# Thirty-nine instead of thirty-three first-product blocks made ahead, quarters dealt evenly, and the last activation emitted where its block ends

## The chip, the cores and the metric

The kernel runs on one core of a Trainium2 chip. The metric is the device time of one execution in microseconds (us), lower is better. The engines are TensorE (PE in the rows, with its weight loads as PEld), VectorE (DVE), ScalarE (ACT), GpSimd (POOL) and SyncE (SP); ACTq, SPq and POOLq are the sequencers that issue their transfers.

## The reference, cut to what matters

One encoder layer; what matters here is its last part, a retrieval layer that picks 16 of 16,384 experts for each of 1,024 tokens and each of 8 heads.

```python
def chunk(xc):                                   # a chunk of 128 tokens
    ...
    top_s, pos = lax.top_k(cand_s, PEER_TOPK)
    e = jnp.take_along_axis(cand_i, pos, axis=-1)          # which experts
    g = jax.nn.softmax(top_s, axis=-1).astype(xc.dtype)    # their gates
    u = peer_u[e]
    h = jax.nn.gelu(jnp.einsum('cd,chkd->chk', xc, u))     # first product
    return jnp.einsum('chk,chkd->cd', g * h, peer_v[e])    # second product
```

## The kernel before

The first 790 us (attention, convolution, projections, the start of the retrieval) are the same in both kernels. From there the tokens are handled in two ways.

**Gathered tokens.** The first 384 tokens (3 tiles of 128) are done by gathers: GpSimd issues an indirect load of 128 rows of `peer_u` or `peer_v` (512 KB, line 1152) and VectorE takes one product-and-sum over it (line 1185 for u, line 1197 for v). There are 768 such gathers in all. In the stretch below the token row that they are multiplied with lies in SBUF (`QB`); in the main loop it lies in PSUM (`ga`).

**Dense tokens.** The other 640 tokens go through all 16,384 experts, in 128 blocks of 128 experts. A block needs three things: H, the gelu of the first product (48 TensorE matmuls of 320 columns, as fp32 values split in a high and a low part, in groups of 12 called quarters here); the gates, which a gate group turns into a dense matrix for 4 tokens at a time (160 groups); and the second product of gated H with `peer_v`.

**The stretch made ahead** (lines 1398 to 1410, 862 to 1370 us). While the gate groups run, `ustep` (line 1343) makes the first product of some blocks ahead, one quarter of TensorE work after each gate group. A gate group is 3 matmuls of 512 columns (`gdiff`, lines 1080 to 1083), two ScalarE activations (`gprep`), 4 matmuls that show as 8 records (`gmat`, line 1098) and 4 ScalarE copies of 128 columns into `gblk` (`gevac`, line 1108). After eight groups ScalarE issues four transfers `GD<-gblk` (line 1111). There are five `gblk` buffers and four are used by each eight groups, so the next eight soon wait for those transfers to land. The H of a finished block gets its gelu in the middle of the next block (line 1241) and is written to HBM (`HDm`). K0 = 33 blocks are listed for this, spread over the 128 (set `US`); KM = K0 - 2 = 31 of them are done by `ustep`, 124 quarters, so they run out while 24 gate groups are left. The last gelu stands after the loop (line 1408). `kadv` deals VectorE's work in the same loop: the key selection first, then gathers, with a cost of GCOST = 3.0 each against a credit that grows with each step.

**The hand-over** (1364 to 1388 us). The two remaining listed blocks are made at once (96 matmuls), while SyncE loads what the main loop needs first: in its queue stand, in this order, the write of the last H (line 1409), a `peer_uT` block (line 1216), a stored H (line 1469), two gate loads (line 1449) and the first two `peer_v` blocks (line 1453). ScalarE and GpSimd split `peer_v` into `vh` and `vl`, and the main loop begins.

**The main loop** (lines 1594 to 1624, 127 rounds, 1388 to 2971 us). Round i does the second product of block i in three slots. Each slot holds a `rotate` (6 matmuls of 512 columns into `prot`, which VectorE adds to X, line 1557), one or two `accum` (3 matmuls of 512 columns each into PSUM that stays) and, by `ugroup`, one quarter of the first product of a block that was not made ahead. Then come the gathers of that slot, on VectorE behind the add. There is one `prot` buffer, so the next slot's `rotate` waits for VectorE's add. The 95 blocks that were not made ahead have 380 quarters for 381 slots.

The program order within each engine is as the code emits it; nothing reorders it.

Of the kernel before, what the change touches and what calls it, by code (L numbers as in the profile page):

```python
# [31 lines left out]
NK = 128  # L32
# [7 lines left out]
TB = 32  # L40
GCH = 4
NPERS = 4
K0 = 33
WIN = 2
NVI = 3
NO2 = 2
GPE = 1.4
GCOST = 3.0
KT = 2
GLAST = 1  # L50
FD = 2
# [20 lines left out]
def peer_block(tc, I, out):  # L72
    nc = tc.nc
    ctx = ExitStack()
    V, A, G, PE, SY = nc.vector, nc.scalar, nc.gpsimd, nc.tensor, nc.sync
# [51 lines left out]
    with ExitStack() as fr:  # L127
# [55 lines left out]
        with ExitStack() as st:  # L183
            a_ = st.enter_context(tc.tile_pool(name="A", bufs=1))
            ps = st.enter_context(tc.tile_pool(name="psA", bufs=2, space=PSUM))
# [306 lines left out]
        with ExitStack() as st:  # L492
            b_ = st.enter_context(tc.tile_pool(name="B", bufs=1))
            ps = st.enter_context(tc.tile_pool(name="psB", bufs=1, space=PSUM))
# [266 lines left out]
            for u in range(NU + 4):  # L761
                g = (u + 4) // 4
# [58 lines left out]
    TD = ND * P  # L821
    KM = K0 - KT
    SD = dram.tile([NT, P, 2 * PH, NK], F32, name="SD")
    GD = dram.tile([TD // TB, P, NK, TB], F32, name="GD")
    HDm = dram.tile([K0, P, TD], F32, name="HDm")
    HND = dram.tile([NG, P, D], F32, name="HND")
# [12 lines left out]
    up = u_.enter_context(tc.tile_pool(name="up", bufs=1))  # L839
# [41 lines left out]
    def hbank(shape, name):  # L881
        hb["n"] += 1
        return (psh if hb["n"] % 2 else psu).tile(shape, F32, name=name, tag="h", bufs=1)
# [320 lines left out]
    gat = Gather()  # L1204
    US = sorted({0, 1, 2, *(int(2 + j * (NK - 2) / (K0 - 2)) for j in range(K0 - 2))})
    UI = {c: j for j, c in enumerate(US)}
    assert len(US) == K0, len(US)
    ngat = NG * 256
# [5 lines left out]
    def uload(i):  # L1214
        raw = uu.tile([P, DC, P], F32, name="ur", tag="raw", bufs=2)
        SY.dma_start(raw[:], I["peer_uT"][i])
        RAW["u", i] = raw
# [4 lines left out]
    def usplit(i):  # L1222
        raw = RAW.pop(("u", i))
        uh = uu.tile([P, DC, P], F32R, name="uh", tag="uh", bufs=2)
        ul = uu.tile([P, DC, P], F32R, name="ul", tag="ul", bufs=2)
        split(uh[:], ul[:], raw[:], hi_eng=HE(i), lo_eng=V if i in UI and UI[i] > KM else G)
        UW[i] = (uh, ul)

    def useg(i, hps, d0, d1):
        uh, ul = UW[i]  # L1230
        for dc in range(d0, d1):
            for st3 in range(3):
                for j, (a, b) in enumerate(segs):
                    PE.matmul(hps[:, j, :b - a], (uh, uh, ul)[st3][:, dc, :], HN[(0, 1, 0)[st3]][:, dc, a:b],  # L1234
                              start=dc == 0 and st3 == 0, stop=dc == DC - 1 and st3 == 2)
        if d1 == DC:
            UW.pop(i)

    def gelu_(hps, pool, bufs):
        ho = pool.tile([P, TD], F32, name="ho", tag="ho", bufs=bufs)  # L1240
        A.activation(ho[:].rearrange("p (a b) -> p a b", a=len(segs)), hps[:, :len(segs), :SW], AF.Gelu_apprx_tanh)  # L1241
        return ho


    korder = [3, 4, 5, 0, 6, 7, 1, 2]
    ks = dict(n1=0, n2=0, gen=None, ld=0, credit=0.0, last="")
# [36 lines left out]
    def k_gat():  # L1283
        if not ks.get("gat") or not gat.ready():
            return None
        gat.adv(1)
        return GCOST

    def kstep():
        order = [("gen", k_gen), ("topk1", k_topk1), ("gat", k_gat)]  # L1290
# [9 lines left out]
    def kadv(us, dt):  # L1300
        clk["t"] += dt
        ks["credit"] = min(ks["credit"] + us, 6.0)
        while ks["credit"] > 0:
            c = kstep()
            if c is None:
                return
            if c == HOLD:
                break
            ks["credit"] -= c
# [30 lines left out]

    ust = dict(i=0, seg=0, hps=None, prev=None)

    def ustep():
        i = ust["i"]
        if i >= KM:
            return 0.0
        if i == 0 and ust["seg"] == 0:
            uload(US[0])
            uload(US[1])
            usplit(US[0])  # L1350
        sg = ust["seg"]
        if sg == 0:
            ust["hps"] = hbank([P, 2, 512], "hps")
        useg(US[i], ust["hps"], 2 * sg, 2 * sg + 2)
        if sg == 1 and ust["prev"] is not None:
            ho = gelu_(ust["prev"], up, 1)
            SY.dma_start(HDm[i - 1], ho[:])
        if sg == 1 and i < KM:
            usplit(US[i + 1])
            if i + 2 < K0:  # L1360
                uload(US[i + 2])
        ust["seg"] += 1
        if ust["seg"] == 4:
            ust["seg"] = 0
            ust["i"] += 1
            ust["prev"] = ust["hps"]
        return 1.65
# [32 lines left out]
    while True:  # L1400
# [4 lines left out]
            break  # L1405
        dt = max(dt + GPE * did, KB)
        kadv(dt, dt)
    ho = gelu_(ust["prev"], up, 1)
    SY.dma_start(HDm[KM - 1], ho[:])
    while ks["n2"] < len(korder):  # L1410
        clk["t"] += 2.0
        kstep()
# [2 lines left out]
    with ExitStack() as vs:  # L1415
# [40 lines left out]
        def vsplit(i):  # L1456
            raw = RAW.pop(("v", i))
            vh = vp.tile([P, D], F32R, name="vh", tag="vh", bufs=WIN + 1)
            vl = vp.tile([P, D], F32R, name="vl", tag="vl", bufs=WIN + 1)
            split(vh[:], vl[:], raw[:], lo_eng=G)  # L1460
            CH[i] = (vh, vl)
# [4 lines left out]
        def hload(i):  # L1466
            if i in UI and i not in HO and i < NK:
                HO[i] = hfree.pop(0)
                SY.dma_start(HO[i], HDm[UI[i]])
# [17 lines left out]
        def uhalf(i, hf, ps, d0=0, d1=DC):  # L1487
            a, b = segs[hf]
            uh, ul = UW[i]
            for dc in range(d0, d1):  # L1490
                for st3 in range(3):
                    PE.matmul(ps[:, :b - a], (uh, uh, ul)[st3][:, dc, :], HN[(0, 1, 0)[st3]][:, dc, a:b],  # L1492
                              start=dc == 0 and st3 == 0, stop=dc == DC - 1 and st3 == 2)
            if hf and d1 == DC:
                UW.pop(i)

        def ubank():
            return psv.tile([P, 512], F32, name="hps", tag="h", bufs=1)

        def ugelu(ho, hf, ps):  # L1500
            a, b = segs[hf]
            A.activation(ho[:, a:b], ps[:, :b - a], AF.Gelu_apprx_tanh)  # L1502

        def loads(i):
            if 0 <= i < NK:
                if i % GCH == 0:
                    gload(i)
                vload(i)


        ulist = [i for i in range(NK) if i not in UI]
        ug = dict(g=0, split=0, load=0, ps=None)

        def uahead():
            m = ug["g"] // 4
            if ug["split"] < min(m + 2, len(ulist)):
                usplit(ulist[ug["split"]])
                ug["split"] += 1
                if ug["load"] < len(ulist):
                    uload(ulist[ug["load"]])  # L1520
                    ug["load"] += 1

        def ugroup():
            m, q = divmod(ug["g"], 4)
            if m >= len(ulist):
                return
            i, (hf, d) = ulist[m], divmod(q, 2)
            if ug["split"] <= m:
                uahead()
            if d == 0:  # L1530
                ug["ps"] = ubank()
            uhalf(i, hf, ug["ps"], d * DC // 2, (d + 1) * DC // 2)
            if d == 1:
                if hf == 0:
                    HO[i] = hfree.pop(0)
                ugelu(HO[i], hf, ug["ps"])
            ug["g"] += 1

        def uready(i):
            while i not in UI and ulist.index(i) >= ug["g"] // 4:  # L1540
                ugroup()
# [19 lines left out]
        gat.to_psum(ga[:])  # L1561
        for i in range(KM + 2, K0):
            uload(US[i])
# [6 lines left out]
        for i in range(KM, K0):  # L1570
# [7 lines left out]
            ho = vp.tile([P, TD], F32, name="hm", tag="al", bufs=WIN + 1)[:]  # L1578
# [17 lines left out]
        for i in range(NK - 1):  # L1596
            nx = i + 1
            ng = gat0 + -(-(ngat - gat0) * min(nx, nb) // nb) - gat.nc
            gs = [0] * 3
            for j in range(ng):  # L1600
                gs[SPOTS[j % len(SPOTS)]] += 1
            hload(nx)
            if len(hfree) > 1:
                hload(i + 2)
            loads(i + 2)
            vsplit(nx)
            uahead()
            rs_ = [w for w in range(len(rot)) if i % WIN == w % WIN]
            rotate(rs_[0], i, False)
            accum(i, (0,))  # L1610
            ugroup()
            gat.adv(gs[0])
            rotate(rs_[1], i, False)
            accum(i, (1,))
            ugroup()
            uready(nx)
            amake1(nx)
            gat.adv(gs[1])
            amake2(nx)
            rotate(rs_[2], i, False)  # L1620
            accum(i, (2, 3))
            ugroup()
            gat.adv(gs[2])
            CH.pop(i - WIN, None)
        accum(NK - 1, range(len(pers)))
# [71 lines left out]
```

## Time and profile before

| | us |
|---|---|
| median of 3 runs | 3005.8 |
| lowest and highest of them | 3000.25 and 3015.49 |
| the profiled execution, its own time | 3001.72 |
| its span, first to last instruction | 2999.9 |
| TensorE busy in the span | 2796.1 (93%) |
| VectorE busy | 2464.3 (82%) |
| GpSimd busy | 1951.2 (65%) |
| ScalarE busy | 1148.3 (38%) |

Of the profiled execution 1.8 us lie around the span. Busy shares are means over stages with different limits, so the rows further down are taken stage by stage. Matmuls overlap in the records (one of 512 columns shows 0.39 us, and the next starts 0.23 us after it), so distances between starts are used for TensorE, not durations.

### The profile page before, as it was taken

The page shows a single profiled execution, that of the slowest core. Times are in us where ns is not written, and L with a number is a line of the kernel's source. Part 1 is how long each engine was busy: PE and PEld are TensorE (multiplying, and loading weights), DVE is VectorE, ACT ScalarE, POOL GpSimd, SP SyncE. Part 2 cuts the span into 40 slices and gives each one's busy share as a digit, 9 for nine tenths or more (in the row PEclk, how much of TensorE's full clock was granted, in tenths as well). Part 3 has the DMA queues.
Part 4 walks back from the last instruction along what each step waited for, and adds up shares of the span by engine and source line. Part 5 has one row for each costly group of instructions (what it writes and reads, how often), then busy time and mean ns, then how long its engine had stood idle before and what let it go on. Part 6 is the DMA issues. An engine that isn't in the chain of part 4 may idle for free.

```text
span 2999.9 us, 44538 instructions
## 1 busy us (share of the span) xinstructions
PE 2796.1 (93%) x16048; PEld 2476.5 (83%) x16048; DVE 2464.3 (82%) x4465; ACT 1148.3 (38%) x2376; POOL 1951.2 (65%) x1557
## 2 busy tenths in 40 slices
PE   7878899899999899988999999999999999999997
PEld 6767778699978788867888888888888888888886
DVE  5888998457667867874999988898999999899898
ACT  3216566243577577673222222222222222222222
POOL 2577842104445757774777777777777777777775
PEclk9999999999999999999999999999999999999999
DMA  3111000044334567576889898999899999999896
GB/s 125 51 68 36 8 1 15 31 145 131 109 122 163 205 245 265 196 288 246 340 330 344 328 347 334 339 337 355 335 338 335 354 342 340 339 339 340 331 343 230
DMA packets 296720, 710.33 MB, mean 237 GB/s; under 512 B 25265, under 2 KB 135217, under 8 KB 296369
## 3 DMA queue, kind: packets, MB, share of 16 engines
q0 software_dynamic: 110592, 402.70, 35.1%
q1 hardware_dynamic: 156800, 252.85, 25.0%
q10 hardware_dynamic: 29104, 51.91, 4.6%
q8 instruction: 126, 2.06, 0.3%
q14 instruction: 98, 0.79, 0.1%
HBM read 640.46 MB, written 66.91 MB: 236 GB/s over the span
## 4 chain that ended last, share of the span: by engine, by line
PE 50%; DVE 21%; DMA 12%; issue 8%; POOL 4%; ACT 4%; ACTq 1%; SPq 0%; POOLq 0%; DVEq 0%
PE hps L1492 12%; PE hps L1234 5%; PE prot L122 4%; PE prot L123 3%; PE prot L124 3%; DMA rows<-peer_u,ei 3%; DMA vr<-peer_v 3%; DVE y L146 3%; PE pg L1098 3%; DMA rows<-peer_v,ei 3%; DVE ga L1197 2%; PE acc L122 2%; PE acc L124 2%; PE acc L123 2%; DVE ho L1475 2%
## 5 line engine op out<-in xcount | busy, mean ns | idle before, releaser
L1492 PE MATMUL hps<-HN,uh 128*128 128x320 f32 x3072 | 682.9, 310 | 9.9 <-ACT ho L1241 5.3
L1492 PEld LDWEIGHTS hps<-HN,uh 128*128 128x128 f32 x3072 | 530.3, 188 | 42.9 <-issue 5.5
L1492 PE MATMUL hps<-HN,ul 128*128 128x320 f32 x1536 | 476.1, 310 | 0.6 <-POOL ul L119 0.6
L1197 DVE SCALAR_TENSOR_TENSOR ga<-rows,aa,ga 128x1024 f32<-128x1024 f32 x330 | 423.9, 1285 | 23.3 <-DMA rows<-peer_v,ei 16.7
L1152 POOL DMA_INDIRECT rows<-peer_u,ei x339 | 360.3, 1063 | 109.5 <-issue 57.9
L119 POOL TENSOR_TENSOR vl<-vr,vh 128x1024 fp32r<-128x1024 f32 x128 | 308.9, 2413 | 154.0 <-ACT vh L116 110.8
L1152 POOL DMA_INDIRECT rows<-peer_v,ei x330 | 325.4, 986 | 110.6 <-issue 64.1
L1185 DVE SCALAR_TENSOR_TENSOR QB<-rows,ga 128x1024 bf16<-128x1024 f32 x271 | 329.5, 1216 | 30.0 <-DMA rows<-peer_u,ei 25.8
L122 PE MATMUL prot<-vh,ah 128*128 128x512 f32 x762 | 308.3, 405 | 29.2 <-DVE X L1557 26.9
L119 POOL TENSOR_TENSOR ul<-ur,uh 128x1024 fp32r<-128x1024 f32 x127 | 323.2, 2545 | 2.6
L1557 DVE TENSOR_TENSOR X<-X,prot 128x512 f32<-128x512 f32 x384 | 262.0, 682 | 68.1 <-PE prot L124 66.7
L123 PE MATMUL prot<-vl,ah 128*128 128x512 f32 x762 | 301.2, 395 | 0.4 <-POOL vl L119 0.4
L124 PE MATMUL prot<-vh,al 128*128 128x512 f32 x762 | 297.6, 390 | 0.0
L1492 PEld LDWEIGHTS hps<-HN,ul 128*128 128x128 f32 x1536 | 289.2, 188 | 0.9 <-POOL ul L119 0.9
L1502 ACT ACTIVATE ho<-hps 128x320 f32<-128x320 f32 x128 | 55.8, 436 | 486.4 <-PE hps L1492 486.4
L1108 ACT COPY gblk<-pg 128x128 f32<-128x128 f32 x640 | 175.9, 441 | 97.0 <-PE pg L1098 72.5
L116 ACT CAST vh<-vr 128x1024 fp32r<-128x1024 f32 x128 | 133.7, 1045 | 202.1 <-DMA vr<-peer_v 193.3
L1234 PE MATMUL hps<-HN,uh 128*128 128x320 f32 x992 | 210.0, 334 | 0.0
L124 PE MATMUL acc<-vh,al 128*128 128x512 f32 x512 | 199.6, 390 | 0.0
L122 PE MATMUL acc<-vh,ah 128*128 128x512 f32 x512 | 199.6, 390 | 0.0
L123 PE MATMUL acc<-vl,ah 128*128 128x512 f32 x512 | 199.5, 390 | 0.0
L122 PEld LDWEIGHTS prot<-vh,ah 128*128 128x128 f32 x762 | 143.3, 188 | 64.6 <-DVE X L1557 44.5
(270 smaller groups left out, 6556.6 us busy)
## 6 DMA issues: line engine op xcount, KB each, us to landing
ur<-peer_uT SPq DMA_DIRECT2D x128, 512.0 KB, 4.2
vr<-peer_v SPq DMA_DIRECT2D x128, 512.0 KB, 7.8
GD<-gblk ACTq DMA_DIRECT2D x80, 512.0 KB, 5.2
gl<-GD SPq DMA_DIRECT2D x64, 640.0 KB, 8.0
wqr<-peer_wq SPq DMA_DIRECT2D x32, 512.0 KB, 3.9
HDm<-ho SPq DMA_DIRECT2D x31, 320.0 KB, 2.6
s<-SD SPq DMA_DIRECT2D x64, 128.0 KB, 2.9
ho<-HDm SPq DMA_DIRECT2D x22, 320.0 KB, 4.6
```

Source lines behind the costliest of these rows:

```text
L116: A.copy(hi, src)
L119: lo_eng.tensor_tensor(lo, src, f(hi), op=ALU.subtract)
L122: PE.matmul(ps, ah, bh, start=start, stop=False)
L123: PE.matmul(ps, ah, bl, start=False, stop=False)
L124: PE.matmul(ps, al, bh, start=False, stop=stop)
L1108: A.copy(gblk[b][k][:, :, q * 4:q * 4 + 4].rearrange("p i t -> p t i"), pg[:, :, k * w:k * w + w])
L1152: G.indirect_dma_start(out=r, out_offset=None, in_=I["peer_v" if ph else "peer_u"], in_offset=bass.IndirectOffsetOnAxis(ap=ge[t][:, k:k + ...
L1185: V.scalar_tensor_tensor(jk, r, 1.0, h, op0=ALU.mult, op1=ALU.mult, accum_out=self.hh[t][:, k:k + 1])
L1197: V.scalar_tensor_tensor(to, r, self.aa[t][:, k:k + 1], to, op0=ALU.mult, op1=ALU.add)
L1234: PE.matmul(hps[:, j, :b - a], (uh, uh, ul)[st3][:, dc, :], HN[(0, 1, 0)[st3]][:, dc, a:b], start=dc == 0 and st3 == 0, stop=dc == DC - 1 ...
L1492: PE.matmul(ps[:, :b - a], (uh, uh, ul)[st3][:, dc, :], HN[(0, 1, 0)[st3]][:, dc, a:b], start=dc == 0 and st3 == 0, stop=dc == DC - 1 and ...
L1557: V.tensor_tensor(X[:, NG + t, n:n + 512], X[:, NG + t, n:n + 512], pr, op=ALU.add)
```

## The change

K0 goes from 33 to 39, so KM goes from 31 to 37 and `ustep` has 148 quarters. `US` is spread anew, and 89 blocks stay for the main loop, with 356 quarters. A new `uslot` stands in the main loop where `ugroup` stood and calls it only when the share of quarters that is due by this slot is not yet made. The last gelu and its write move into a function `ulast`, which `ustep` calls as soon as it has no block left. Gathers that are dealt after the key selection count 2.0 against the credit instead of 3.0.

```diff
-K0 = 33
+K0 = 39
@@
 GCOST = 3.0
+GCOST2 = 2.0
@@
-        return GCOST
+        return GCOST if ks["n2"] < len(korder) else GCOST2
@@
+    def ulast():
+        if ust["prev"] is not None:
+            ho = gelu_(ust["prev"], up, 1)
+            SY.dma_start(HDm[KM - 1], ho[:])
+            ust["prev"] = None
+
     def ustep():
         i = ust["i"]
         if i >= KM:
+            ulast()
             return 0.0
@@
-    ho = gelu_(ust["prev"], up, 1)
-    SY.dma_start(HDm[KM - 1], ho[:])
+    ulast()
@@
-        ug = dict(g=0, split=0, load=0, ps=None)
+        ug = dict(g=0, split=0, load=0, ps=None, slot=0)
@@
+        def uslot():
+            ug["slot"] += 1
+            if ug["g"] < -(-4 * len(ulist) * ug["slot"] // (3 * (NK - 1))):
+                ugroup()
@@
             accum(i, (0,))
-            ugroup()
+            uslot()
```

The other two calls of `ugroup` in the round become `uslot` in the same way.

What this does to the order is seen at three places. On TensorE, the end of the stretch made ahead: `pg` is a gate group's product, `dg` and `dq` belong to the group after it, and `hps` on line 1234 (1235 after) is a quarter. Before:

```order
L1083 MATMUL dg<-selg,L_5328 128x512
L1098 MATMUL pg<-o_14199,o_14197 128x128 x4
L1098 MATMUL pg<-o_14214,o_14212 128x128 x4
L1492 MATMUL hps<-HN_5301,uh 128x320
L1492 MATMUL hps<-HN_5302,uh 128x320
```

and after the change:

```order
L1235 MATMUL hps<-HN_5301,ul 128x320 x2
L1099 MATMUL pg<-o_14566,o_14564 128x128 x4
L1235 MATMUL hps<-HN_5301,uh 128x320 x2
L1235 MATMUL hps<-HN_5302,uh 128x320 x2
L1235 MATMUL hps<-HN_5301,ul 128x320 x2
```

The last 24 groups stood alone; now a quarter of 12 matmuls stands behind each of them, the last one included.

On ScalarE at the same place, before:

```order
L1089 ACTIVATE o_14212<-dq 128x512
L1091 ACTIVATE o_14214<-dg 128x512
L1108 COPY gblk<-pg 128x4x32 x8
L1111 DMA GD<-gblk 128x1024 x4
L1241 ACT_TABLE_LOAD
L1241 ACTIVATE ho<-hps 128x640
L1144 COPY ga<-QB 128x1024
L116 CAST uh<-ur 128x1024
```

and after the change:

```order
L1090 ACTIVATE o_14564<-dq 128x512
L1092 ACTIVATE o_14566<-dg 128x512
L1109 COPY gblk<-pg 128x4x32 x4
L1242 ACTIVATE ho<-hps 128x640
L1109 COPY gblk<-pg 128x4x32 x4
L1112 DMA GD<-gblk 128x1024 x4
L1145 COPY ga<-QB 128x1024
L117 CAST uh<-ur 128x1024
```

The last gelu moved ahead of the last group's copies and of the four transfers; its table load is no longer here (there are as many table loads in all).

On TensorE in the main loop, first slot of round 5; `acc` is the `accum`, `hps` the quarter. Before:

```order
L124 MATMUL prot<-vh,al 128x512
L122 MATMUL acc_14253<-vh,ah 128x512
L123 MATMUL acc_14253<-vl,ah 128x512
L124 MATMUL acc_14253<-vh,al 128x512
L1492 MATMUL hps<-HN_5301,uh 128x320
L1492 MATMUL hps<-HN_5302,uh 128x320
```

and after the change:

```order
L125 MATMUL prot<-vh,al 128x512
L123 MATMUL acc_14619<-vh,ah 128x512
L124 MATMUL acc_14619<-vl,ah 128x512
L125 MATMUL acc_14619<-vh,al 128x512
L123 MATMUL prot<-vh,ah 128x512
L124 MATMUL prot<-vl,ah 128x512
```

The quarter between one `rotate` and the next is gone in this slot; 24 slots are like it, one in every fifth round (8 in each of a round's three places).

## Rows read from the trace of the kernel before

**Rows 1.** By stage: stretch, length, busy PE, PEld, DVE, ACT, POOL; clock, DMA share, GB/s.

```profile
862.00:1303.00 441.00, 417.11 (x2842) 376.51 (x2841) 334.16 (x1195) 311.07 (x869) 284.68 (x230) 0.99 0.60 210
1303.00:1365.00 62.00, 46.28 (x262) 33.13 (x260) 38.91 (x50) 45.31 (x141) 34.22 (x22) 0.89 0.69 250
1365.00:1388.00 23.00, 16.63 (x97) 16.28 (x97) 3.04 (x4) 9.18 (x15) 1.87 (x1) 0.85 0.77 260
1388.00:2971.00 1583.00, 1557.94 (x8361) 1380.72 (x8361) 1429.03 (x1778) 388.35 (x548) 1230.41 (x918) 1.00 0.91 337
```

**Rows 2.** TensorE in order of time: start, us, instruction, count, idle before and releaser.

```profile
1275.38 1.05 PE L1098 MATMUL pg<-o,o 128*128 128x128 f32 x8
...
1280.33 0.94 PE L1098 MATMUL pg<-o,o 128*128 128x128 f32 x7
...
1300.09 1.05 PE L1098 MATMUL pg<-o,o 128*128 128x128 f32 x8
...
1303.39 1.05 PE L1098 MATMUL pg<-o,o 128*128 128x128 f32 x8
...
1363.34 1.16 PE L1098 MATMUL pg<-o,o 128*128 128x128 f32 x8 [0.37 <-ACT o L1091]
```

**Rows 3.** Chain of work that ended last, within the lone gate groups: start, us, what.

```profile
1321.91 6.37 DMA GD<-gblk
...
1341.04 11.29 DMA GD<-gblk
...
1364.54 1.02 ACT gblk L1108 x4
```

**Rows 4.** All engines in order of time at the hand-over, 1365 to 1388 us.

```profile
1365.30 2.39 ACTq L1111 DMA_DIRECT2D GD<-gblk  x3
1367.72 1.28 ACT L1241 ACT_TABLE_LOAD   x1 [2.17 <-issue]
1369.02 0.70 ACT L1241 ACTIVATE ho<-hps 128x640 f32<-128x640 f32 x1
...
1369.82 0.87 PE L1492 MATMUL hps<-HN,uh 128*128 128x320 f32 x2 [5.32 <-ACT ho L1241]
...
1371.78 1.23 DVE L119 TENSOR_TENSOR ul<-ur,uh 128x1024 fp32r<-128x1024 f32 x1 [28.07 <-ACT uh L116]
...
1376.53 3.76 SPq L1453 DMA_DIRECT2D vr<-peer_v  x2
...
1385.84 0.31 PE L1492 MATMUL prot<-HN,ul 128*128 128x320 f32 x1
1387.70 0.47 PE L122 MATMUL prot<-vh,ah 128*128 128x512 f32 x1 [1.55 <-issue]
```

**Rows 5.** Who waited for whom in the main loop: us in total, times, longest.

```profile
DVE X L1557 <- PE prot L124: 66.7, 99, 3.5
...
PEld prot L122 <- DVE X L1557: 35.9, 64, 1.7
...
DVE ho L1475 <- ACT ho L1502: 1.8, 1, 1.8
```

**Rows 6.** Two slots of the main loop in order of time, TensorE and VectorE.

```profile
1455.24 0.46 PE L1492 MATMUL hps<-HN,uh 128*128 128x320 f32 x2
...
1455.31 0.68 DVE L1557 TENSOR_TENSOR X<-X,prot 128x512 f32<-128x512 f32 x1
...
1456.99 0.39 PE L122 MATMUL prot<-vh,ah 128*128 128x512 f32 x1
...
2592.07 1.22 DVE L1185 SCALAR_TENSOR_TENSOR QB<-rows,ga 128x1024 bf16<-128x1024 f32 x1 [1.74 <-DMA rows<-peer_u,ei]
...
2592.57 0.45 PE L1492 MATMUL hps<-HN,uh 128*128 128x320 f32 x2
...
2594.48 0.68 DVE L1557 TENSOR_TENSOR X<-X,prot 128x512 f32<-128x512 f32 x1
...
2595.21 0.50 PE L122 MATMUL prot<-vh,ah 128*128 128x512 f32 x1 [0.72 <-DVE X L1557]
```

More of the change, by code (lines that the diff above doesn't have):

```diff
@@ L1614, in peer_block @@
             accum(i, (1,))
-            ugroup()
+            uslot()
             uready(nx)
@@ L1621, in peer_block @@
             accum(i, (2, 3))
-            ugroup()
+            uslot()
             gat.adv(gs[2])
```

## Prediction

> **What bounds the kernel now.** I read the busy time by stage first, then each stage's waits. In the main loop TensorE is busy 1557.94 of 1583 us at full clock, VectorE 1429.03, and the DMA engines 0.91 of the time [rows 1]: three resources within a tenth of each other, TensorE the first of them. What it waits for there is one thing, VectorE's add that frees `prot`: 35.9 us in 64 waits [rows 5]. VectorE in turn waits for TensorE before 99 of its 380 adds, 66.7 us [rows 5]. The other adds start late because VectorE is still at a gather's product, sometimes one that itself waited for its rows (the second slot of [rows 6]).
>
> In the stretch made ahead a step (gate group and quarter) takes 3.30 us, from 1300.09 to 1303.39 [rows 2], and TensorE is the bound (417.11 of 441 us busy [rows 1]). When the quarters run out, at 1303.39, 24 groups are left, and they take until 1363.34 + 1.16 = 1364.5 [rows 2]: 61.1 us, 2.55 each. TensorE is busy 46.28 of those 62 us, at a granted clock of 0.89 [rows 1]. The chain says why: it goes through the landings of `GD<-gblk`, 6.37 and 11.29 us of two of them [rows 3], since the copies of the next eight groups wait for the buffers.
>
> **Term 1, 24 quarters more in the stretch: +23.1 us there.** The order puts one quarter behind each of the 24 lone groups, so these become 24 steps: 24 x 3.30 = 79.2 us. Every eighth step is longer, because ScalarE issues four transfers in it and then waits for the buffers: 1275.38 to 1280.33, 4.95 us, 1.65 more than a plain one [rows 2]. Three of them fall into 24 steps: +5.0. So 84.2 us in place of 61.1, +23.1. The bounds are 79.2 (+18.1, no such extra) and 93.2 (+32), where each landing takes 11.29 us as in [rows 3] and two steps cover 6.6 of it, leaving 4.7 three times over. I take the middle one, since the row of 4.95 is of the very pattern that is now continued. What goes with it is hidden: GpSimd casts six blocks more and VectorE does nine gathers more (77 instead of 68 before the hand-over) in a stretch where they are busy 34.22 and 38.91 of 62 us, and six more writes of H on SyncE's queue meet a DMA share of 0.69 [rows 1].
>
> **Term 2, the hand-over: -0.9 us, and +1 for the clock.** Before, the last group ends at 1364.5 and the main loop's first matmul starts at 1387.70 [rows 4]: 23.2 us, of which 18.0 come after the last gelu has ended (1369.02 + 0.70). In the order after, no table load stands there any more and the gelu is ahead of the last copies, so TensorE goes on some 1.0 us after its last quarter instead of 5.32 after its last group [rows 4]. But that isn't the path. The 96 matmuls ended at 1386.1, and the loop waited for `vl`, made of a `peer_v` block whose load was issued at 1376.53; that load stands on SyncE's queue behind a load that needs `ul` (1371.78), which follows ScalarE's cast behind the gelu [rows 4]. Now four copies (1.02 us [rows 3]) and the issue of transfers (2.39 us [rows 4]) are put between the gelu and that cast. So: 0.2 for the gelu to start, 0.70 for it, 3.4 for what moved behind it, 18.0 as before: 22.3 us, -0.9. If the loads came early enough, only the 96 matmuls would count: at 0.147 each (a quarter's 1.75 us [rows 6] by 12) 14.1, with 1.0 ahead and 1.5 behind 16.6 us (-6.6). If the transfers land late it may be as much as a landing's spread of 5 us worse [rows 3]. I take -0.9, the sum of rows. TensorE then idles some 7 us ahead of the loop; with the idle of 5.32 us the clock was 0.85 on average in the hand-over [rows 1, 4], so I add 1 us for matmuls at half clock.
>
> **Term 3, the main loop: -17 us.** 24 quarters leave it. One takes 1455.24 to 1456.99, 1.75 us [rows 6]: 42.0 us of TensorE work. But a quarter also covers VectorE's add. In the first slot shown the add ends at 1455.99, and without the quarter the next `rotate` could start only then, 0.75 us after the `accum` ended at 1455.24; in the second it ends at 2595.16, 2.59 us after, and even the quarter doesn't cover it [rows 6]. I read the same distance, with 0.05 us for the signal, at each of the 24 slots that lose their quarter; these two are the first of them and the worst. It goes from 0 to 2.65 us, 19.9 us in all, of which 3.0 are waited already. That takes 16.9 of the 42.0 and leaves 25.1. Of this, part is waited for later. After each such slot TensorE stands 1.05 us further ahead, and only at 99 of 380 adds was VectorE idle and able to follow [rows 5]. Bounds: nothing more is lost (VectorE's 66.7 us of waiting absorb it all), or all 25.1. I put it at 8, nearer to nothing, because the nine gathers that left take 9 x 1.22 = 11.0 us (the product at 2592.07 in [rows 6]) off VectorE's own work. So 17 us are gained, with bounds of 0 and 37 (37 if the 16 slots with a single `accum` lose only the 0.3 us of an add that starts at once).
>
> One row speaks for room on TensorE: its weight loads are busy 1380.72 of 1583 us, 87% [rows 1]. The Trainium skill ("Perfetto Trace Analysis", Identifying the Most-Contended Engine) says that matmul occupancy is a poor measure of TensorE's headroom, and that the weight loads' share and the arithmetic rate should be used instead. By that rule TensorE has 13% to spare, something else paces the loop, and term 3 is nothing (+23.2 in all); by the waits above it is the pace for all but 36 us (+6.2). The trace so far is against the rule: TensorE waits for nothing else. It stands with the second rival.
>
> Other edits. Five blocks instead of one have their last quarter in the slot just ahead of their use; the one time that this happens now, VectorE waits 1.8 us for the gelu [rows 5], so four more cost at most 7 us and I take nothing, since that wait lies on VectorE. HBM traffic of the loop falls by about 1% (six `peer_uT` blocks and nine gathers less, six stored H more), as its time does.
>
> **Sum.** +23.1 - 0.9 + 1 - 17 = +6.2 us on the profiled execution's 3001.7: 3007.9, so 3008. The median of the three runs is 4.1 us above that execution, and their spread of 15 us is as large as 0.5% (about what a measurement of this kernel can tell from no change); the range reaches up for it.
>
> **Rivals.**
> *The quarters come out of the loop nearly whole.* VectorE follows at once, since it waits 66.7 us for TensorE now. With the loop's bound, +23.1 - 0.9 + 1 - 37 = -14; with the short hand-over of 16.6 us, -20. About 2984. It decides if a removed quarter costs less than 0.3 us of waiting. For it: TensorE is the busiest. Against: VectorE at 90% and the transfers at 0.91 [rows 1] have little to give.
> *The loop's pace is VectorE's (slower).* Each missing quarter turns into as long a wait for the add, the loop takes as long as before, and the other terms stand alone, +23.2: 3025. It decides when the loop gives back under 8 us. For it: the late adds [rows 5, 6]. Against: TensorE waits only 36 us in 1583 [rows 5].
> *The filler doesn't hide the landings.* The long landings of the lone groups [rows 3] stay exposed as at term 1's upper bound, 9 us more than taken: 3017. It would show as eighth steps of 8 us instead of 5.
>
> **Chances.** Forecast 0.63, the quarters whole 0.14, VectorE's pace 0.15, landings exposed 0.08. The forecast's own range is 2995 to 3018 from its bounds; I widen it to 2988 and 3022, which leaves out most of the first rival and most of the second. Faster by over 0.5% has the first rival and a little of the forecast, 0.15; slower has the second and half of the third, 0.19; within 0.5% the rest, 0.66.
>
> **What would show it.** Right: 24 more steps of 3.3 us with three of about 5; the first main-loop matmul about 22 us later than 1387.70, after some 7 us of idle TensorE; a loop of about 1566 us, with 17 to 25 us more of waiting for the add than 35.9. A loop shorter by over 30 us, or no shorter at all, would be the first or the second rival. What I would have missed altogether: VectorE or GpSimd starving a step in the stretch, or waits for stored H in the loop.

## The result and the profile after

| | us |
|---|---|
| before, median of 6 runs | 3003.82 (2998.59 to 3015.49) |
| after, median of 6 runs | 3079.56 (3068.53 to 3083.62) |
| after over before | 1.025, 95% interval 1.0234 to 1.0266 |
| profiled execution after, its span | 3078.0 (before 2999.9) |

The change makes the kernel slower by 2.5%. The forecast was 3008, "within 0.5%", with a range of 2988 to 3022: wrong.

By stage, the kernel after, in the columns of [rows 1]:

```profile
1303.00:1365.00 62.00, 58.66 (x404) 52.78 (x402) 52.33 (x55) 40.31 (x112) 53.09 (x32) 1.00 0.76 269
...
1388.00:1420.00 32.00, 24.17 (x130) 22.52 (x129) 6.09 (x9) 9.74 (x16) 7.77 (x4) 0.84 0.73 240
1420.00:2971.00 1551.00, 1468.49 (x7705) 1290.55 (x7705) 1336.06 (x1692) 362.09 (x507) 1150.01 (x866) 0.98 0.88 327
```

Up to 1388 us it goes nearly as forecast: the 62 us that held 46.28 us of TensorE work [rows 1] now hold 58.66, and the clock there went from 0.89 to 1.00. The last row is where the forecast fails (the main loop itself now runs on to 3052 us). In [rows 1] TensorE was busy 98% of the main loop at a clock of 1.00. Now it is busy 95% at 0.98, though it has less to do.

The gate groups on TensorE, and the start of the main loop (last row), to be held against [rows 2] and [rows 4]:

```profile
1305.29 1.05 PE L1099 MATMUL pg<-o,o 128*128 128x128 f32 x8
1309.66 1.05 PE L1099 MATMUL pg<-o,o 128*128 128x128 f32 x8
1312.95 1.05 PE L1099 MATMUL pg<-o,o 128*128 128x128 f32 x8
...
1360.13 1.05 PE L1099 MATMUL pg<-o,o 128*128 128x128 f32 x8
1365.57 1.05 PE L1099 MATMUL pg<-o,o 128*128 128x128 f32 x8
...
1413.81 0.80 PE L123 MATMUL prot<-vh,ah 128*128 128x512 f32 x1 [6.00 <-ACT hm L1509]
```

A step takes 3.29 us, an eighth one 4.37 (1305.29 to 1309.66) to 5.44 (1360.13 to 1365.57), and the loop starts at 1413.81 instead of 1387.70 [rows 4], 26.1 us later.

To compare main loops I take the distance from the first `rotate` of the loop to the first one behind it, and set beside it the work in it: the number of matmuls times the distance between adjacent starts, 0.147 us at 320 columns and 0.2285 at 512. I call the rest waiting. It holds TensorE's idle time and, behind a long wait, what its matmuls lose at the lower of the clock's two levels (1.2 instead of 2.4 GHz). Before: 1586.2 = 1540.2 + 46.0. After: 1637.9 = 1498.0 + 140.0, in which the weight loads stand idle for 122.8 us; so some 17 us of the 140 are slow matmuls. So the span's 78.1 us are

- the loop starts later: +26.1
- 24 quarters less work in it: -42.2
- more waiting in it: **+94.0**
- the rest: +0.2.

Of the 140 us, 92.5 lie in 18 of the 127 rounds, those that wait over 2 us beyond their work: rounds 11 and 19, 35 and 39, 59, 79 and 83, 99 and 103, 119 and 123 and seven smaller ones. They come in clusters about 20 rounds apart. The eleven that are named wait 4.6 to 11.4 us each, 74 us in all. Who waits for whom in the loop after, as in [rows 5]:

```profile
ACT vh L117 <- DMA vr<-peer_v: 218.3, 32, 15.6
POOL vl L120 <- ACT vh L117: 212.8, 43, 24.3
PEld prot L123 <- DVE X L1569: 44.7, 52, 2.5
PEld hps L1499 <- ACT ho L1509: 31.4, 14, 8.2
PEld hps L1499 <- POOL ul L120: 22.3, 6, 3.8
PEld hps L1499 <- ACT QB L1509: 14.7, 4, 9.8
```

TensorE's wait for VectorE's add, on which the forecast turned, grew from 35.9 [rows 5] to 44.7 us only. New, but for 3.4, 0.9 and 5.1 us before, are waits of 31.4, 22.3 and 14.7 us for ScalarE's gelu (`ho` and `QB` are the buffers of H) and GpSimd's `ul`. The first two rows say what is behind them: a `peer_v` block that lands up to 15.6 us after ScalarE is ready to cast it. Four of the five longest pieces in the whole chain that ended last are such landings (start, us, what):

```profile
1650.54 13.89 DMA vr<-peer_v
1855.25 14.27 DMA vr<-peer_v
2728.14 16.59 DMA vr<-peer_v
2985.54 18.13 DMA vr<-peer_v
```

Among the five longest pieces before, one was of this kind, of 10.19 us.

One such round after, followed back along the chain (start, us, what):

```profile
2673.95 0.50 DVE ho L1482
...
2674.46 0.37 SPq L1456
...
2674.88 13.10 DMA vr<-peer_v
...
2689.18 0.92 POOL vl L120
...
2691.50 2.94 POOL ul L120
...
2694.48 3.03 PE hps L1499 x10
```

and ScalarE and SyncE's queue in it, in order of time:

```profile
2662.51 12.32 SPq L1456 DMA_DIRECT2D gl<-GD  x2
2674.88 5.07 SPq L1460 DMA_DIRECT2D vr<-peer_v  x2
...
2688.06 1.05 ACT L117 CAST vh<-vr 128x1024 fp32r<-128x1024 f32 x1 [8.72 <-DMA vr<-peer_v]
2689.01 1.04 ACT L117 CAST uh<-ur 128x1024 fp32r<-128x1024 f32 x1
2689.96 0.43 ACT L1509 ACTIVATE QB<-hps 128x320 f32<-128x320 f32 x1
```

Read it from the top. In every fourth round SyncE issues two gate loads and then the `peer_v` load. The second gate load has no free buffer until VectorE's product at 2673.95, and `peer_v` is behind it in the queue: both are issued 12 us late. Then `peer_v` takes 13.1 us to land. ScalarE runs in order, so the cast holds the gelu behind it, which frees the one `hps` bank, and the cast of `uh`, from which GpSimd makes `ul`. TensorE goes on at 2694.48, when `ul` is there, after waits of 1.19 and 3.49 us, and at first slowly: its 10 matmuls take 3.03 us, 0.30 each instead of 0.147, at a granted clock of 0.50 from 2694 to 2697.

This holds round by round. There are 31 rounds with gate loads behind the loop's start. In eleven of them the cast of `peer_v` comes 13.0 to 18.2 us after the load's issue, and these are the eleven rounds named above; in the other 20 it comes 7.3 to 11.6 us after, and none of them waits over 3.2 us.

The same place of the pattern in the kernel before, SyncE, ScalarE and GpSimd:

```profile
1572.12 0.38 SPq L1449 DMA_DIRECT2D gl<-GD  x1
1572.60 0.60 SPq L1453 DMA_DIRECT2D vr<-peer_v  x1
...
1581.09 1.05 ACT L116 CAST vh<-vr 128x1024 fp32r<-128x1024 f32 x1 [6.94 <-DMA vr<-peer_v]
...
1566.96 2.41 POOL L119 TENSOR_TENSOR vl<-vr,vh 128x1024 fp32r<-128x1024 f32 x1 [0.21 <-ACT vh L116]
1569.34 2.40 POOL L119 TENSOR_TENSOR ul<-ur,uh 128x1024 fp32r<-128x1024 f32 x1
```

The hold is there too (the first gate load was issued 22 us earlier), but the load is cast 8.5 us after its issue. GpSimd made `vl` and `ul` one after the other just before, 4.8 us in which it issued no gather, so that the transfer engines were nearly free when the second gate load came. In the bad round after, GpSimd had no `ul` to make and the gathers ran on.

What the two share is seen in the packets of the two queues (q0: gathers, q1: SyncE's and ScalarE's), before, from 1556 to 1561 us (gathers and a gate load in flight), from 1573 to 1576 (the gate load nearly alone) and from 1577 to 1584 (gathers and `peer_v`); columns: packets, MB, share of 16 engines:

```profile
q0 software_dynamic: 460, 1.69, 84.7%
q1 hardware_dynamic: 472, 0.24, 16.5%
...
q1 hardware_dynamic: 1266, 0.65, 78.2%
q0 software_dynamic: 21, 0.09, 8.5%
...
q1 hardware_dynamic: 409, 1.52, 54.2%
q0 software_dynamic: 369, 1.33, 47.8%
```

Where both have work all the time, the two queues get about as many packets through as each other (460 and 472; 369 and 409), although those of the first pair differ in size. The gate loads come in packets of 512 bytes and the gathers and `peer_v` mostly in 4096, so beside gathers the gate load gets 0.24 MB in 5 us, and alone 0.65 in 3. `peer_v`, issued at 1572.60 behind the gate load, has its packets from about 1577 on, when the gate load's are through. Not every stretch is so even: in e3 below, from 1590 to 1595, the counts are 342 and 1054. The Trainium skill ("DMA: Bandwidth & Descriptors", Queues, rings and completion order) says that each transfer engine goes round the queues that have work and drains a whole packet, typically some 9 to 17 descriptors, before it switches. The trace agrees with the taking of turns, with the numbers of the two even stretches; whether a packet of the profile is one of the page's is not shown.

### The profile page after: what moved, and what is told of

Same layout as the page of the kernel before. It is cut to its first block, busy times and chain, and to the rows that moved or that the text cites. A ratio compares the mean times of both kernels' runs of the same rounds, so it can differ in the third digit from the quotient of the medians.

```text
span 3078.0 us, 44533 instructions
## 1 busy us (share of the span) xinstructions
PE 2812.7 (91%) x16042; PEld 2488.3 (81%) x16048; DVE 2456.3 (80%) x4465; ACT 1143.7 (37%) x2364; POOL 1956.0 (64%) x1563
## 4 chain that ended last, share of the span: by engine, by line
PE 44%; DVE 19%; DMA 15%; issue 10%; POOL 5%; ACT 4%; ACTq 1%; SPq 0%; POOLq 0%; another core or an unknown queue 0%; DVEq 0%
PE hps L1499 9%; DMA vr<-peer_v 6%; PE hps L1235 5%; DMA rows<-peer_u,ei 4%; PE prot L123 3%; DVE y L147 3%; PE pg L1099 3%; PE prot L124 3%; PE prot L125 3%; DMA rows<-peer_v,ei 2%; DVE ga L1198 2%; DVE ho L1482 2%; POOL rows L1153 2%; DVE PT L120 1%; DVE QB L1186 1%
## 5 line engine op out<-in xcount | busy, mean ns | idle before, releaser
L1499 PE MATMUL hps<-HN,uh 128*128 128x320 f32 x2880 | 651.6, 313 | 40.5 <-ACT ho L1509 25.7
L1499 PEld LDWEIGHTS hps<-HN,uh 128*128 128x128 f32 x2880 | 505.2, 192 | 75.2 <-ACT ho L1509 31.4
L1499 PE MATMUL hps<-HN,ul 128*128 128x320 f32 x1440 | 452.6, 314 | 20.7 <-POOL ul L120 20.7
L1186 DVE SCALAR_TENSOR_TENSOR QB<-rows,ga 128x1024 bf16<-128x1024 f32 x264 | 321.1, 1216 | 31.1 <-DMA rows<-peer_u,ei 19.1
L1499 PEld LDWEIGHTS hps<-HN,ul 128*128 128x128 f32 x1440 | 276.3, 192 | 22.3 <-POOL ul L120 22.3
L1235 PE MATMUL hps<-HN,uh 128*128 128x320 f32 x1184 | 250.4, 334 | 0.0
L117 ACT CAST vh<-vr 128x1024 fp32r<-128x1024 f32 x128 | 133.8, 1045 | 237.1 <-DMA vr<-peer_v 218.3
L1235 PEld LDWEIGHTS hps<-HN,uh 128*128 128x128 f32 x1184 | 193.8, 190 | 21.5 <-issue 0.6
```

Of the source, the lines that this page charges most:

```text
L117: A.copy(hi, src)
L1186: V.scalar_tensor_tensor(jk, r, 1.0, h, op0=ALU.mult, op1=ALU.mult, accum_out=self.hh[t][:, k:k + 1])
```

## The experiments

Three theories. **Phase:** a block takes four quarters. Before, with a quarter in all slots but one, three blocks took exactly four rounds, and so did a pair of gate loads: the pattern was locked, in a phase that did little harm. With 356 quarters dealt evenly over 381 slots it slips by one quarter in five rounds, and runs through all four phases in about 20 (TensorE's matmuls ahead of each round, counted in the trace, show it). **Cover:** the mechanism of my prediction, that the slots without a quarter leave VectorE's add open. **Loads:** six more loads of stored H disturb the queues.

The table has all runs; "cast" is ScalarE's wait for `peer_v` in the loop. Times of one run stand without an interval. Beside them the kernel before took 3009.1 us (e1 to e4), 3000.5 (e5 to e8), 3009.2 (e9 to e11) and 3017.4 (e12); the ratios below are against these.

| run | kernel | time, us | loop starts | work | waits | cast |
|---|---|---|---|---|---|---|
| | before | 3003.8 | 1387.7 | 1540.2 | 46.0 | 193 |
| | after | 3079.6 | 1413.8 | 1498.0 | 140.0 | 218 |
| e1 | after, pattern locked | 3018.6 | 1412.4 | 1498.0 | 81.0 | 205 |
| e2, e5 | after, `peer_v` first | 2978.0; 2976.7 | 1416.0 | 1498.0 | 36.0; 28.5 | 14; 4 |
| e3 | before, one quarter ahead | 3166.5 | 1397.8 | 1538.5 | 202.2 | 236 |
| e4 | before, two ahead | 2994.6 | 1395.8 | 1536.7 | 34.7 | 226 |
| e10 | before, three ahead | 3083.0 | 1397.4 | 1534.9 | 123.2 | 176 |
| e6 | before, `peer_v` first | 2967.7 | 1388.2 | 1540.2 | 8.7 | 0.4 |
| e7 | e3 and `peer_v` first | 2971.5 | 1397.6 | 1538.5 | 7.9 | 0.5 |
| e12 | e10 and `peer_v` first | 2970.2 | 1395.8 | 1534.9 | 12.1 | 19 |
| e8 | after, 33 blocks | 3004.5 | 1391.7 | 1540.2 | 45.0 | 200 |
| e9 | e3, no gathers in the loop | (3934.5) | 1396.6 | 1538.5 | 1.7 | 11 |
| e11 | e6, second gate load later | 2967.9 | 1391.5 | 1540.2 | 9.2 | 0 |

**e1: the six blocks without the slip.**

```diff
-    US = sorted({0, 1, 2, *(int(2 + j * (NK - 2) / (K0 - 2)) for j in range(K0 - 2))})
+    US = sorted({0, 1, 2, *(int(2 + j * (NK - 2) / (K0 - 8)) for j in range(K0 - 8))})
+    US = sorted({*range(8), *(8 + i for i in US if i < NK - 8)} - {NK - 1})
@@
-            if ug["g"] < -(-4 * len(ulist) * ug["slot"] // (3 * (NK - 1))):
+            if ug["slot"] > 24:
                 ugroup()
```

> The changed kernel, with its 39 blocks made ahead chosen otherwise: blocks 0 to 7 and then one in four as in the kernel before, and the quarters not dealt evenly but three in every round from round 8 on. Work on TensorE is that of the changed kernel (1498 us in the main loop). Phase theory (the evenly dealt quarters drift against the gate loads, which come every fourth round, and every 20 rounds or so meet them badly): the drift is gone, the loop's waits fall from 140 to 45 to 65 us, total 2985 to 3010 us. Cover theory (my prediction's mechanism: a slot without a quarter leaves VectorE's add open): 24 slots lack a quarter as before, all in rounds 0 to 7 now; the 94 us of added waits sit in these rounds (about 4 us a slot), total about 3078. Load theory (39 loads of stored H instead of 33 disturb the queues, wherever they lie): waits stay at 120 to 150 us, total 3060 to 3080.

Its waits are split as both the first two theories say. TensorE's weight loads waiting in rounds 0 to 8 (first row) and in the rest of the loop:

```profile
PEld prot L123 <- DVE X L1570: 34.5, 22, 5.8
...
PEld prot L123 <- DVE X L1570: 25.7, 44, 2.6
```

Behind the ninth round only one round waits over 2 us, and 36 us are left there, where the kernel before has 38 in the same rounds and the kernel after 134. The slip's stalls are gone. It isn't the slip alone that was taken out, though: behind round 10 the stored blocks lie one in four again, as in the kernel before, so this run doesn't speak against the load theory. In rounds 0 to 8, where 24 slots lack a quarter, 44.9 us are waited, by the first row mostly for VectorE's add. The kernel before waits 7.9 us there, so 37 us are more: 1.5 us a slot, of the quarter's 1.75. The clock in these rounds is 0.88 (third number from the end), so part of it is slow matmuls:

```profile
1412.00:1540.00 128.00, 101.84 (x392) 77.38 (x393) 106.43 (x170) 22.65 (x30) 88.83 (x71) 0.88 0.91 331
```

So the cover is real too, and in one heap it takes back most of the work that was removed. Because of these 45 us the total is 9 us above what the phase theory expected.

**e2 and e5: `peer_v` ahead of the gate loads.**

```diff
         def loads(i):
             if 0 <= i < NK:
+                vload(i)
                 if i % GCH == 0:
                     gload(i)
-                vload(i)
```

> The changed kernel with two lines exchanged: in every fourth round the peer_v load is issued on SyncE's queue ahead of the two gate loads rather than behind them. Phase theory: in the bad rounds of the changed kernel ScalarE is held at the cast of peer_v, whose load lands 13 us after its issue because it stands behind the second gate load; issued ahead it lands in 4 to 7 us, the stalls of over 2 us (92 us in 18 rounds) fall to 20 to 50 us, total 3000 to 3040 us, unless the gate loads now come late for VectorE's product, when the stalls move there (wait of VectorE on the gate load over 60 us, total 3060 to 3090). Cover theory and load theory: the order of these loads matters little, 3070 to 3085 us.

> The changed kernel with the peer_v load issued ahead of the gate loads, as in e2, timed. If e2's one time holds: 2972 to 2984 us, 0.989 to 0.994 of the kernel before, faster than both kernels. If e2 was a lucky run: 3000 us or more.

Timed: 2976.7 us, 0.9922 of before (0.9908 to 0.9937). ScalarE's wait for `peer_v` falls from 218.3 to 3.9 us, and no wait of TensorE for a gelu or `ul` is left. In e5's loop:

```profile
PEld prot L123 <- DVE X L1569: 24.6, 30, 2.7
ACT vh L117 <- DMA vr<-peer_v: 3.9, 1, 3.9
```

Two lines exchanged take 112 us of waiting away, with the slip, the missing quarters and all 39 stored blocks in place. Neither of the other theories allows that, and it is more than the phase theory expected of e2 (3000 to 3040 us): the new order also takes waits that the kernel before has.

**e3, e4 and e10: the kernel before in the other three phases.** One, two or three quarters are issued between the hand-over and the loop; 33 blocks, nothing else.

```diff
         nb = NK - GLAST
+        for _ in range(1):
+            ugroup()
```

> The kernel before, with one quarter issued between the hand-over and the main loop, so that all quarters, and with them the splits and loads of peer_u, stand one slot earlier against the gate loads for the whole loop; 33 blocks ahead, every slot but two with a quarter, as before. Phase theory: the kernel before stood in a good phase by chance; if this phase is the bad one, the stall of 5 to 7 us comes in most of the 31 rounds in which gates are loaded, total 3080 to 3180 us; if it is a harmless one, 3000 to 3010. At least one of the shifts by 1, 2 and 3 quarters gives more than 3050. Cover theory and load theory: neither the cover nor the number of loads is changed, 3000 to 3010 us for every shift.

> The kernel before, with two quarters issued between the hand-over and the main loop: the same as the shift by one, two slots earlier. Phase theory: either 3000 to 3010 us (a harmless phase) or 3080 to 3180 us (the round in which GpSimd has no low half of peer_u to make falls on the round in which the gates are loaded), and the bad shift shows peer_v landing 12 us or more after its issue in rounds with a gate load. Cover theory and load theory: 3000 to 3010 us.

> The kernel before with three quarters ahead of the main loop, the last of the four phases (none: 3000 us, one: 3166, two: 2995). The changed kernel passes through all four in a period of about 20 rounds, its bad rounds in clusters; 92 us in 18 such rounds against 165 us in 31 rounds in the bad phase says that a good half of its rounds with gate loads are bad, so that this phase should cost too: 3040 to 3170 us. If only one phase in four is bad: 2995 to 3010 us.

The kernel before loses some 160 us by one quarter's shift, without any stored block more. Waits in the loop of e3:

```profile
ACT vh L116 <- DMA vr<-peer_v: 235.8, 31, 10.3
PEld hps L1492 <- POOL ul L119: 110.0, 31, 3.8
```

31 of each, as many as rounds with gate loads. TensorE's weight loads stand idle 150.9 of the 202.2 us; the rest are matmuls at the lower level (the clock is 0.96 over the loop). In e10 the stall shows on another engine, VectorE:

```profile
PEld prot L122 <- DVE X L1557: 84.7, 63, 4.8
```

In e4 ScalarE waits nearly as long as in e3 (226 us), and yet TensorE waits less than before, so the length of ScalarE's wait doesn't tell. From issue to cast, in the median of the 32 rounds with gate loads, `peer_v` takes 7.9 us before, 12.9 in e3, 8.8 in e4 and 9.7 in e10.

The mean of the four phases' waits is (46.0 + 202.2 + 34.7 + 123.2) / 4 = 101.5 us; a kernel that slips through all of them, with some 20 us for the cover (below), should wait about 121. The kernel after waits 140, and not where this would have it. Counted from the quarters made, e3's phase falls on six of its gate loads; the rounds behind them (19, 39, 59, 79, 99, 119) wait 4.6 to 6.5 us, 34 us in all, as in e3. The other five late rounds (11, 35, 83, 103, 123), 40 us, lie in other phases. In four of them the gates are loaded for a group of four blocks whose first has a stored H (12, 36, 104, 124). Outside e3's phase eight rounds with gate loads are like that, and four are late; of the 17 others one is. In the kernel before no such block but block 0 begins a group of four. So the new places of the stored H are a second suspect for when `peer_v` comes late, and no run tells them from the slip: e1 moved both.

**e7 and e12: bad phases with `peer_v` first.** The exchange of e2 in the kernels of e3 and e10.

> The kernel before with one quarter ahead of the loop (e3: 3166 us, 202 us of waits in the loop) and the peer_v load ahead of the gate loads. If the stalls in the bad phase come from peer_v's place behind the second gate load: waits of 30 to 60 us in the loop, 2985 to 3015 us. If they come from the gates' own landing, or from GpSimd's low half of peer_u being late for another reason (102 us of waits on it in e3): 3060 to 3170 us.

> The kernel of e10 (three quarters ahead of the main loop, 123 us of waits in it, 85 us of them in front of VectorE's add) with the peer_v load issued ahead of the gate loads. If the order of these loads is the cause in this phase too, whatever engine the stall shows on: 5 to 20 us of waits in the loop, 2963 to 2980 us. If this phase has a cause of its own: over 60 us of waits, 3020 us or more.

Both lose their stalls: 202.2 to 7.9 us (30 to 60 were expected) and 123.2 to 12.1. The loop of e7, in which `ul` no longer appears:

```profile
PEld prot L122 <- DVE X L1557: 3.0, 5, 1.0
ACT vh L116 <- DMA vr<-peer_v: 0.5, 1, 0.5
```

So the order of the loads is the cause in both, also where the stall shows on VectorE.

**e9: the bad phase without gathers.** The three `gat.adv(gs[...])` of the round are taken out, and all the gathers run behind the loop; only the loop is read.

```diff
             ugroup()
-            gat.adv(gs[0])
             rotate(rs_[1], i, False)
```

> The kernel of e3 (one quarter ahead of the loop, the bad phase) with the gathers of peer rows taken out of the main loop and all done behind it, so that its total is far longer and only the main loop's waits are read. If peer_v lands late because the gathers' packets share the transfer engines with the gate loads (e3: 512-byte packets move at some 50 KB a us beside gathers, 150 to 280 without): peer_v's cast waits under 60 us in the loop (e3: 236) and TensorE's waits on ul, ho and QB together fall from 118 to under 30 us. If the second gate load's wait for a free buffer, with peer_v queued behind it, is enough by itself: the cast still waits 120 us or more and TensorE 60 us or more.

The first row is ScalarE's wait in the loop, the second SyncE's for the gate load's buffer:

```profile
ACT vh L116 <- DMA vr<-peer_v: 10.6, 25, 1.7
...
SPq L1449 <- DVE ho L1475: 247.1, 21, 11.8
```

SyncE still holds `peer_v` behind the second gate load for up to 11.8 us, and it does no harm: the cast comes 6.2 us after the issue (median of the 32) instead of 12.9 in e3. So the hold alone isn't enough; the gathers must be in flight. Without them GpSimd and VectorE are freer as well, so for TensorE's waits the run shows less than for the landing.

**e6: what the order gives to the kernel before, and e11: the second gate load later still.**

```diff
-        def gload(i):
-            for hf in range(2):
+        def gload(i, halves=(0, 1)):
+            for hf in halves:
@@
+                vload(i)
                 if i % GCH == 0:
-                    gload(i)
-                vload(i)
+                    gload(i, (0,) if i else (0, 1))
@@
             amake1(nx)
+            if nx % GCH == GCH - 1 and nx + 1 < NK:
+                gload(nx + 1, (1,))
```

> The kernel before (33 blocks ahead, a quarter in every slot) with the peer_v load issued ahead of the gate loads. If the loads' order is worth something by itself, also in the good phase: some 10 us of the loop's 46 us of waits go, 2985 to 2997 us, and the six blocks are then worth 10 to 20 us (26 us later at the loop's start, 42 us less work in it). If the order only undoes the bad phase, which this kernel does not have: 2999 to 3008 us, and the six blocks with the new order are worth 20 to 30 us.

> The kernel before with peer_v's load first, then the first gate load, and the second gate load issued only when its buffer is about to be free (behind the next block's product), so that it holds back no other load on SyncE's queue. If the hold of the loads behind the second gate load still costs something after e6: 2958 to 2966 us. If e6 has taken all there is (8.7 us of waits are left in its loop): 2964 to 2975 us. If the second half now lands too late for VectorE's product: 2975 to 3010 us, with waits of VectorE on the gate load over 40 us.

e6 runs in 2967.7 us, 0.9894 of before (0.9878 to 0.9909), faster than both kernels and below both expectations: 37 of the 46 us that the loop waited before came of the order too. The loop is TensorE's nearly alone:

```profile
1388.00:2937.00 1549.00, 1544.55 (x8373) 1383.99 (x8374) 1329.37 (x1781) 385.75 (x549) 1236.82 (x918) 1.00 0.92 345
```

e11 (ratio 0.9868, 0.9846 to 0.9889) can't be told from it, as expected if e6 has taken what there was.

**e8: the small edits alone**, with `K0 = 33` in the kernel after.

> The changed kernel with 33 blocks made ahead instead of 39, which leaves of the change the price of a gate copy among the last groups, the place of the last activation and the rule that deals the quarters, by which 380 quarters in 381 slots stand one in each slot as in the kernel before. Phase theory and my prediction: these edits are worth nothing by themselves, 2995 to 3010 us. If the dealing or the hand-over did the harm: over 3030 us.

3004.5 us, 1.001 of before (1.0001 to 1.0019), with the loop's waits at 45.0. The price of a gather (the expectation's "gate copy"), the place of the last gelu and the new rule cost nothing to speak of.

## Why the prediction was wrong, point by point

- **Term 1, the stretch: right.** Steps of 3.30 were forecast and 3.29 measured, three eighth ones of 4.95 against 4.37, 4.36 and 5.44. The 24 steps take 84.7 us against 84.2, and the last quarter ends at about 1390.0 instead of the forecast 1387.6, mostly because the first of them starts 1.9 us later than in the kernel before. Two landings stayed nearly hidden. The third did not: it is in the chain (first row), the two steps behind that eighth one take 5.10 and 3.97 us, and the three together are 4.6 us over plain steps, about what the third rival has for one landing (4.7). So its mechanism came once, not three times.

```profile
1359.18 11.04 DMA GD<-gblk
...
1393.51 6.25 DMA GD<-gblk
```

- **Term 2, the hand-over: nearly right.** From the last quarter to the loop's first matmul 23.8 us against 22.3, with 6.0 us of idle TensorE against 7. In part this is luck: the chain goes through the landing of the last `GD<-gblk` (second row above), not through ScalarE's cast and `ul`. Both terms together start the loop 26.1 us later, against 22.2 by the two sums of the forecast.
- **Term 3, the loop: -17 forecast, +51.7 measured; near in what it priced.** With `peer_v` first the phase matters little (8.7, 7.9 and 12.1 us of waits in e6, e7 and e12), and the loops can be compared without it: e6 1548.9 = 1540.2 + 8.7, e5 1526.5 = 1498.0 + 28.5. Work falls by 42.2 and 19.8 us come back as waits, nearly all for the add (27 in e2), where I had 42.0 and 24.9 (16.9 and 8). The net is -22 and -15 in the two, -17 was forecast. The whole change in this order costs 2976.7 - 2967.7 = 9.0 us, and my sum was +6.2.
- **The step that failed: "TensorE waits for nothing else", and the other edits taken at nothing.** I took the loop's waits from one state of a repeating pattern, and counted the 24 quarters as work and cover. I didn't ask what the quarters' places do to the other engines. Dealt evenly, 356 quarters slip against the gate loads, and six more stored blocks lie elsewhere; `peer_v`, queued behind the gate loads, then comes late in eleven rounds, and some 74 us come of that (94.0 less 20). Measured by the order of the loads, it is the same: `peer_v` first takes 111.5 us of waiting from the kernel after and 37.3 from the kernel before, 74.2 more. Some 17 us of the 140 are matmuls at the lower clock, where I took the loop at full clock. The row that warned was in the view I had read, and I passed over it because TensorE didn't wait there:

```profile
ACT vh L116 <- DMA vr<-peer_v: 193.3, 31, 7.8
```

  My list of what could be missed named a starved step and waits for stored H. Neither came, though the places of the stored H may have had a part (above).
- **The second rival** ended on the right side, at 3025, for a wrong reason. Only 9 of the 94 us are more of TensorE's weight-load waits for VectorE's add (35.9 to 44.7), and the loop did give back 22.4 us when the order of the loads was changed (e5 against e6).
- **The rule beside it.** By the weight loads' share, which the Trainium skill ("Perfetto Trace Analysis", Identifying the Most-Contended Engine) recommends beside the arithmetic rate for judging headroom, TensorE had room to spare, and term 3 would be nothing. In e6 the loads are busy 1383.99 of 1549 us, 89%, and TensorE waits 8.7 us; the quarters that left the loop made it 22 us shorter in e5. Here the waits were the better measure.

**Open.** That the order of the loads costs the 74 us is shown (e2, e5, e7, e12). What makes `peer_v` late in one round and not in another is shown for one phase (e3) only: five of the eleven late rounds of the kernel after lie outside it, and whether the places of the stored H or the gathers in flight make those late was not tested. Nor is it shown why two quarters ahead do no harm although ScalarE waits 226 us there, or by which work the late `peer_v` reaches VectorE's add in e10.

## What to carry to other kernels

When an edit changes how often something happens in a loop, look at what else repeats in the loop with another period, on every queue. A pattern that is locked has only one phase in its trace; shifting the old kernel by a step or two, as in e3, e4 and e10, shows what the others cost before the edit is made. In this loop it paid in every phase tried to queue the load that an in-order engine needs soon ahead of those that wait for a buffer or move in small packets. And an engine that waits long without harm, as ScalarE did here for 193 us, is a warning, not a reserve.

## What the hardware showed that I had not expected

With both at work the two queues shared the transfer engines packet for packet (460 and 472 in 5 us), so a load in 512-byte packets got 0.24 MB where the gathers, in 4096-byte ones, got 1.69; without gathers it got 0.65 MB in 3 us. And issuing a load on SyncE can itself be slow: behind the gate loads, with gathers in flight, a `peer_v` issue took 6.21 us in e7 (others some 0.4), with nothing lost by it there:

```profile
1560.84 11.77 SPq L1449 DMA_DIRECT2D gl<-GD  x2
1572.72 6.21 SPq L1453 DMA_DIRECT2D vr<-peer_v  x1
```
